# Both first modulation vectors formed on TensorE, x loaded by token groups, and value tiles moved behind their group's gated tiles

## The chip, the core and the metric

The kernel runs on one core of a Trainium2 chip. The metric is the device time of one execution in microseconds (us). Engines: PE is TensorE (matmuls), DVE is VectorE, ACT is ScalarE, POOL is GpSimd, SP is SyncE, which here only issues DMAs. ScalarE issues a few DMAs too.

## The reference, cut to what matters

One step of a two-layer trunk, in float32, on 128 context tokens and 1024 latent tokens (1152 columns together, feature-major). Each layer begins so:

```
def modulation(cond, w_mod, b_mod):
    m = jax.nn.silu(cond) @ w_mod + b_mod
    return jnp.split(m[:, None, :], 6, axis=-1)

def spatial_gating(uv, g_sgu, w_s, b_s):
    u, v = jnp.split(jax.nn.gelu(uv), 2, axis=-1)
    v = rmsnorm(v, g_sgu)
    ...
    return u * mixed.reshape(b, t, SGU_WIDTH)

def residual_block(x, mods, lp, mixer):
    sh1, sc1, g1, sh2, sc2, g2 = mods
    h = rmsnorm(x, lp['g_mix']) * (1 + sc1) + sh1
    mix, ctx_tensors = mixer(h)
    x = x + g1 * (mix @ lp['w_out'])
```

The normalised and modulated `h` goes through one input projection, whose columns feed neighbourhood attention, latent attention (`cq`, `ckv`, `krope`) and the spatial gating (`u`, `v`). A gated MLP with a depthwise convolution follows. The shift `sh1` and the scale `sc1` of layer 0 must exist before any `h` can be formed. There are two conditions, `c` for the latent tokens and `c_ctx` for the context tokens.

## The kernel before

The 1152 columns are three groups of 384 (G). A float32 product is made of three matmuls per 128-row chunk k (`mm3`, L183 to L185): high weights by high data, high by low, low by high. High parts are cast on ScalarE (L169), low parts are the residue, on VectorE (L171) or on POOL in pieces of 256 columns (L176). With 8 chunks a tile is 24 matmuls.

The opening. The two conditions come in as rows (`ccrow`), TensorE broadcasts them over 128 partitions (`ccb`, L1239), ScalarE applies silu. The shift vector is formed on VectorE: 16 products of 128 x 1024 with a sum along the row (`mod_tile`, L215). The scale vector is formed on TensorE: eight tiles of `wsc` (512 KB each) with a two-column weight (L1271), copied out by ScalarE (`mrow`), turned by eight small transposes (`pmT`). Then `norm_group` for the first group can start.

`norm_group` makes `h` for one group, chunk by chunk: in fused chunks VectorE forms `nt` (L342), ScalarE the high part (L344), VectorE the low one (L345); in the others VectorE (L337), ScalarE (L348, then the cast L169) and POOL (L176). The row factor `R` is statistics on TensorE (L297), a reciprocal root on VectorE (L270 to L278) and a broadcast on TensorE (L302). In layer 0 the squares of the next group (L288, L290) are formed inside the norm of a group.

The gating stage (`sgu`) comes next. For each group it makes two gated tiles (`pj`, weights by tokens, 128 x 384 each), whose gelu goes to `u` (L442). Then come nine value tiles (`pv`, tokens by weights, 128 x 320), three per group; their weights are cast by `tok_weights` to `twh` and `twl` in three loads (`win_v`). A value tile is drained by ScalarE (`vg`, L421, and a square, L423) and by VectorE (`kr`, L429) with POOL (L431). From the sixth value tile on in layer 0, the drain is followed by `mod_some`, products for the next modulation vectors (L235). The groups run in the order 1, 2, 0 in layer 0. In layer 1 the norms are formed in the feed-forward block before, and nothing is called between the tiles. The latent projections follow (`pj` again).

What sets the order: the program is written as below, and a scheduler of the framework then places each engine's instructions in a fixed sequence, by order of writing and by when operands and buffers are expected to be free; `issue_after` holds one instruction behind another. Each engine runs its sequence in order. Buffers come from pools with a fixed number of slots, so a load waits until the reader of the slot's last content is done: the third `win_v` load (L78) waits for the residue of the first. ScalarE's five DMA issues for the gating constants and the table of positions (L401 to L410) stand at the head of `sgu`.

## Time and profile before

| | |
|---|---|
| time, median of 3 runs | 3203.97 us (3203.35 to 3205.04) |
| the profiled execution's own time | 3203.48 us |
| its span in the trace | 3201.3 us |
| TensorE busy | 3114.0 us, 97% of the span |
| VectorE, ScalarE, POOL busy | 57%, 40%, 36% |
| layer 0: first gated matmul to first latent matmul | 45.92 to 119.58 us |
| layer 1: the same | 1628.49 to 1688.77 us |

Times in the rows are counted from the start of the span. A row of a timeline gives the start, the duration, the engine, the line, the operation with what it writes and reads, a count where equal neighbours are put together, and in brackets how long the engine was idle before and what released it. A "granted clock" of 1.00 is TensorE's 2.4 GHz level, 0.50 its 1.2 GHz level; a value between them is a mean over the stretch. An f32 matmul has two records in a count.

### The profile page before, as it was taken

Reading aid. Unit: us, or ns where it says so; the run is one execution under the profiler, and the core shown is the slowest. Engines: PE = TensorE matmul, PEld = TensorE weight load, DVE = VectorE, ACT = ScalarE, POOL = GpSimd, SP = SyncE. Lnnn points to the kernel's source line nnn. Section 1 sums busy time; section 2 is a strip of 40 time slices with the busy share of each in tenths; the row PEclk is TensorE's granted clock in tenths of the full one; section 3 lists DMA queues with packets and bytes.
Section 4 is the critical chain, followed back from the end, with each engine's and each line's share of the span. In section 5 each row is a group of like instructions: output and inputs, shape, how many; then the busy total and the mean of one; then the engine's idle time right before and its main releaser. Section 6 shows DMA issues by size and latency. Waiting matters only on the chain.

```text
span 3201.3 us, 50596 instructions
## 1 busy us (share of the span) xinstructions
PE 3114.0 (97%) x19298; PEld 2961.3 (93%) x19298; DVE 1812.7 (57%) x4908; ACT 1290.5 (40%) x2374; POOL 1155.9 (36%) x1359
## 2 busy tenths in 40 slices
...
GB/s 228 70 152 156 32 10 8 57 122 102 70 82 67 76 82 66 83 78 71 87 100 31 143 93 21 10 19 44 93 36 45 40 44 38 50 42 40 47 40 74
DMA packets 100504, 219.97 MB, mean 69 GB/s; under 512 B 25346, under 2 KB 41890, under 8 KB 100260
## 3 DMA queue, kind: packets, MB, share of 16 engines
...
## 4 chain that ended last, share of the span: by engine, by line
PE 88%; DVE 4%; issue 2%; POOL 2%; ACT 2%; DMA 1%; SPq 0%; DVEq 0%; ACTq 0%; POOLq 0%
PE f L184 11%; PE f L185 11%; PE f L183 11%; PE o L183 6%; PE o L184 6%; PE o L185 5%; PE O L538 5%; PE T L515 5%; PE pj L184 3%; PE pj L183 3%; PE pj L185 3%; PE S L959 2%; PE S L960 2%; PE S L961 2%; PE wo L183 1%
## 5 line engine op out<-in xcount | busy, mean ns | idle before, releaser
L176 POOL TENSOR_TENSOR whl<-wraw,whl 128x256 fp32r<-128x256 f32 (+1 forms) x704 | 549.9, 810 | 1090.6 <-ACT whl L169 883.3
L1090 DVE SCALAR_TENSOR_TENSOR acc<-f,vec,acc 128x1 f32<-128x1 f32 (+3 forms) x1056 | 397.4, 413 | 578.1 <-ACT acc L1086 566.6
L184 PE MATMUL f<-h,whl 128*128 128x384 f32 x2112 | 707.4, 335 | 3.9 <-POOL h L176 3.4
L185 PE MATMUL f<-h,whl 128*128 128x384 f32 x2112 | 706.4, 335 | 0.0
L183 PE MATMUL f<-h,whl 128*128 128x384 f32 x2112 | 705.7, 335 | 0.0
L184 PEld LDWEIGHTS f<-h,whl 128*128 128x128 f32 x2112 | 396.9, 188 | 7.2 <-POOL h L176 5.7
L183 PEld LDWEIGHTS f<-h,whl 128*128 128x128 f32 x2112 | 396.7, 188 | 0.6 <-ACT h L169 0.6
L185 PEld LDWEIGHTS f<-h,whl 128*128 128x128 f32 x2112 | 397.0, 188 | 0.0
L1076 DVE SCALAR_TENSOR_TENSOR x<-o,mod,x 128x384 f32<-128x384 f32 (+2 forms) x512 | 250.9, 514 | 205.6 <-PE o L185 204.8
L169 ACT CAST whl<-wraw 128x1024 fp32r<-128x1024 f32 (+3 forms) x204 | 190.7, 935 | 394.7 <-PE o L185 312.9
L183 PE MATMUL o<-ah,whl 128*128 128x384 f32 x912 | 304.7, 334 | 0.0
L185 PE MATMUL o<-ah,whl 128*128 128x384 f32 x912 | 304.7, 334 | 0.0
L184 PE MATMUL o<-al,whl 128*128 128x384 f32 x912 | 304.7, 334 | 0.0
L1086 ACT ACTIVATE acc<-f,vec 128x384 f32<-128x384 f32 x264 | 175.8, 668 | 156.5 <-PE f L185 151.2
L169 ACT CAST ah<-acc 128x383 fp32r<-128x383 f32 x132 | 67.5, 514 | 410.5 <-POOL acc L1133 410.5
L235 DVE SCALAR_TENSOR_TENSOR junk<-wmh,sc 128x512 bf16<-128x512 f32 x256 | 222.1, 868 | 7.7 <-DMA wmh<-wmodT 3.2
L515 PE MATMUL T<-cst,P 128*128 128x128 f32 x1504 | 201.5, 274 | 1.0 <-ACT P L707 1.0
L1133 POOL TENSOR_TENSOR acc<-acc 128x383 f32<-128x383 f32 x132 | 141.1, 1069 | 149.3 <-DVE acc L1090 149.3
L515 PEld LDWEIGHTS T<-cst,P 128*128 128x128 f32 x1504 | 174.8, 141 | 15.8 <-issue 5.7
L184 PE MATMUL pj<-h,whl 128*128 128x384 f32 x528 | 179.7, 341 | 5.7 <-POOL h L176 3.5
L965 ACT ACTIVATE P<-P,mx 128x1152 f32<-128x1152 f32 x128 | 161.4, 1261 | 55.7 <-DVE mx L962 55.3
L526 ACT COPY PT<-T 128x512 f32<-128x512 f32 (+1 forms) x288 | 154.1, 577 | 70.7 <-PE T L515 70.0
...
## 6 DMA issues: line engine op xcount, KB each, us to landing
...
wmh<-wmodT SPq DMA_DIRECT2D x128, 256.0 KB, 2.8
...
```

What stands on the lines that cost most here:

```text
L169: self.last_hi = self.nc.scalar.copy(hi, src)
L176: self.nc.gpsimd.tensor_tensor(out=lo[:, c], in0=src[:, c], in1=hi[:, c].bitcast(F32), op=ALU.subtract)
L183: mm(ps, wh(k), xh(k), start=(i == 0), stop=False)
L184: mm(ps, wh(k), xl(k), start=False, stop=False)
L185: mm(ps, wl(k), xh(k), start=False, stop=(i == last))
L235: self.nc.vector.scalar_tensor_tensor(out=self.junk[:, 0:512], in0=raw, scalar=1.0, in1=self.sc[c][:, o:o + 512], op0=ALU.mult, op1=ALU.mu ...
L515: nc.tensor.transpose(Tt[:, b * 128:(b + 1) * 128], u["P"][s][:, pc:pc + 128], self.I)
L538: nc.tensor.matmul(u["O"][64 * grp:64 * grp + 64, o0:o0 + n], w, src, start=(u["nop"][grp] == 1), stop=(u["nop"][grp] == u["tot"][grp]))
L965: nc.scalar.activation(out=P, in_=P, func=AF.Exp, bias=mx[:, 2:3], scale=-1.0, accum_out=mx[:, 3:4])
L1076: i = self.nc.vector.scalar_tensor_tensor(out=x[:, c0:c1], in0=ps[:, c0 - g * G:c1 - g * G], scalar=self.m(l, chunk, m, cond), in1=x[:, c0 ...
L1086: nc.scalar.activation(out=acc[:, c:c + G], in_=ps[:, 0:G], func=AF.Identity, scale=w(1), bias=vec[:, V_CB + ft:V_CB + ft + 1])
L1090: return nc.vector.scalar_tensor_tensor(out=acc[:, d:d + n], in0=p[:, s:s + n], scalar=w(i), in1=acc[:, d:d + n], op0=ALU.mult, op1=ALU.add)
```

## The change

Four things are done. The condition's vector is padded with zeros to 32 columns (`ctp`), and both vectors are formed on TensorE, from 16 tiles of 512 KB, with 64 matmuls of 32 x 256 outputs; two copies (ScalarE and VectorE) and four 128 x 128 transposes bring them into columns; `mod_tile` goes. The broadcasts of the conditions are issued after the twelfth tile. `x` is held in three tiles for each group (`XGroup`), group 1 loaded first and group 0 when the first norm has been written; the squares and the row factor of the next group are written after the first value tile of a group (`next0`). And in `sgu`, in both layers, the three value tiles of a group follow its two gated tiles, with the weights' casts written after the first group's gated tiles.

```diff
@@ -124,6 +124,17 @@
         return self._unit(g, k, 1)
 
 
+class XGroup:
+
+
+    def __init__(self, tile, off):
+        self.t, self.off = tile, off
+
+    def __getitem__(self, ix):
+        p, c = ix
+        return self.t[p, c.start + self.off:c.stop + self.off]
+
+
 class Wide:
     def __init__(self, hh, hl):
         self.hh, self.hl = hh, hl
@@ -208,14 +220,6 @@
             nc.scalar.dma_start(out=t, in_=bass.AP(tensor=cc.tensor, offset=cc[i].offset, ap=[[0, 128], [1, 1024]]))
             nc.scalar.activation(out=t, in_=t, func=AF.Silu)
             self.sc.append(t)
-
-    def mod_tile(self, l, t, conds, raw):
-        nc = self.nc
-        for c in conds:
-            i = nc.vector.scalar_tensor_tensor(
-                out=self.junk[:, 0:1024], in0=raw, scalar=1.0, in1=self.sc[c], op0=ALU.mult, op1=ALU.mult,
-                accum_out=self.mpart[:, t, c:c + 1])
-        return i
 
     def mod_half(self, l, n, first, end, buf):
         total = 2 * (end - first)
@@ -431,18 +435,21 @@
                 nc.gpsimd.tensor_tensor(out=self.krtok[:, t, :], in0=r[:, 0:32], in1=r[:, 32:64], op=ALU.add)
             if l == 0 and i >= MOD_FROM:
                 self.mod_some(ins)
+            return end
         for j, g in enumerate(order):
-            if j == 2:
-                W = self.tok_weights(3, 320)
             if norm:
-                norm(g)
+                norm[0](g)
             for i in range(2):
                 ps = self.anybank("pj")[:, 0:G]
                 self.wx(ps, Ws[i], f, g)
                 nc.scalar.activation(out=u[i][:, g * G:(g + 1) * G], in_=ps, func=AF.Gelu_apprx_tanh)
+            if j == 0:
+                W = self.tok_weights(3, 320)
+            for i in range(3):
+                ins = vtile(3 * j + i)
+                if norm and j < 2 and i == 0:
+                    norm[1](g, ins)
         norm = None
-        for i in range(9):
-            vtile(i)
         sm = self.st("sm")
         nc.vector.tensor_scalar(out=sm[:, 0:9], in0=ss[:, 0:9], scalar1=1.0 / 256, scalar2=None, op0=ALU.mult)
         y = self.rsqrt(sm[:, 0:9], 9, self.bank("rsq"))
@@ -1231,84 +1238,78 @@
         for c in range(2):
             nc.sync.dma_start(out=row[c][0:1, 0:1024], in_=io["cc"][c:c + 1, :])
         nc.sync.dma_start(out=self.cst, in_=io["cst"])
-        self.sc = [self.ptp.tile([128, 1152], F32, tag="pt", name="sc")[:, 0:1024] for _ in range(2)]
-        for c in range(2):
-            for j in range(2):
-                ps = self.sbank("ccb")
-                cs = slice(j * 512, (j + 1) * 512)
-                nc.tensor.matmul(ps, self.I[0:1, 0:1].to_broadcast([1, 128]), row[c][0:1, cs], start=True, stop=True)
-                nc.scalar.activation(out=self.sc[c][:, cs], in_=ps, func=AF.Silu)
-        row = None
-        x = [self.slot("x") for _ in range(8)]
+        ct = self.st("ct")
+        nc.sync.dma_start(out=ct[:, 0:16], in_=io["ccT"])
+        xg = {}
 
         def load_x(g):
+            t = [self.slot("xg") for _ in range(3)]
+            xg[g] = [XGroup(t[k // 3], (k % 3 - g) * G) for k in range(8)]
             for k in range(8):
                 cs = slice(g * G, (g + 1) * G)
-                nc.sync.dma_start(out=x[k][:, cs], in_=io["xT"][k, :, cs])
-        raws = []
-        for t in range(8):
-            r = self.slot("wmraw")[:, 0:1024]
-            nc.sync.dma_start(out=r, in_=io["wmodT"][0, t])
-            raws.append(r)
-            if t == 3:
-                load_x(1)
-        ct = self.st("ct")
-        nc.sync.dma_start(out=ct[:, 0:16], in_=io["ccT"])
-        nc.scalar.activation(out=ct[:, 16:32], in_=ct[:, 0:16], func=AF.Silu)
-        self.sq_begin()
-        for c in range(2):
-            for t in range(8):
-                last = self.mod_tile(0, t, (c,), raw=raws[t])
-        raws = None
-        for k in range(8):
-            self.sq_add(k, x[k], 1, nc.gpsimd)
-        pm = self.sbank("pm")
-        q4 = [slice(32 * j, 32 * j + 2) for j in range(4)]
-        for k in range(8):
-            r = self.slot("wmraw")[:, 0:1024]
-            nc.sync.dma_start(out=r, in_=io["wsc"][k])
-            for j in range(4):
-                nc.tensor.matmul(pm[q4[j], 0:256], ct[:, 16 + 2 * k:18 + 2 * k], r[:, j * 256:(j + 1) * 256],
-                                 start=(k == 0), stop=(k == 7))
-            if k == 0:
-                R1 = self.bank("R")
-                y = self.rstd_col(self.sumsq[:, G:2 * G], 0, R1)
-            if k in (5, 6):
-                self.W._load(k - 5)
+                nc.sync.dma_start(out=xg[g][k][:, cs], in_=io["xT"][k, :, cs])
+        load_x(1)
         for l in range(L):
             nc.sync.dma_start(out=self.vec[l], in_=io["vecs"][l])
-        self.bcast(R1, y)
-        R = {1: R1[:, 0:G]}
+        ctp = self.tmp("ctp")[:, 0:256].rearrange("p (k x) -> p k x", x=32)
+        nc.gpsimd.memset(ctp, 0.0)
+        nc.scalar.activation(out=ctp[:, :, 0:2], in_=ct[:, 0:16].rearrange("p (k c) -> p k c", c=2), func=AF.Silu)
+        self.sq_begin()
+        for k in range(8):
+            self.sq_add(k, xg[1][k], 1, nc.vector)
+        R1 = self.bank("R")
+        R = {1: self.rstd(self.sumsq[:, G:2 * G], 0, R1)}
+        pm = [self.bank("pm") for _ in range(2)]
+        for k in range(8):
+            for ch in range(2):
+                r = self.slot("wmraw")[:, 0:1024]
+                nc.sync.dma_start(out=r, in_=io["wsc"][k, :, ch * 1024:(ch + 1) * 1024])
+                for j in range(4):
+                    i = nc.tensor.matmul(pm[ch][32 * j:32 * j + 32, 0:256], ctp[:, k], r[:, j * 256:(j + 1) * 256],
+                                         start=(k == 0), stop=(k == 7))
+            if k == 5:
+                self.sc = [self.ptp.tile([128, 1152], F32, tag="pt", name="sc")[:, 0:1024] for _ in range(2)]
+                with self.tc.issue_after(i.ins):
+                    for c in range(2):
+                        for j in range(2):
+                            ps = self.sbank("ccb")
+                            cs = slice(j * 512, (j + 1) * 512)
+                            nc.tensor.matmul(ps, self.I[0:1, 0:1].to_broadcast([1, 128]), row[c][0:1, cs],
+                                             start=True, stop=True)
+                            nc.scalar.activation(out=self.sc[c][:, cs], in_=ps, func=AF.Silu)
+        row = None
+        self.W._load(1)
         load_x(2)
-        load_x(0)
         pt = self.obank("pmT")
-        for j in range(4):
-            if j % 2 == 0:
-                row = self.tmp("mrow")
-            o = j % 2 * 256
-            nc.scalar.copy(row[0:2, o:o + 256], pm[q4[j], 0:256])
-            for i in range(2):
-                nc.tensor.transpose(pt[:, 4 * j + 2 * i:4 * j + 2 * i + 2], row[0:2, o + i * 128:o + (i + 1) * 128],
-                                    self.I[0:2, 0:2])
-        with self.tc.issue_after(last.ins):
-            nc.vector.tensor_copy(self.mpart[:, 8:16, :].rearrange("p a b -> p (a b)"), pt[:, 0:16])
-        self.mod_finish(0, 0, 2)
+        mrow = self.tmp("mrow")
+        nc.scalar.copy(mrow[:, 0:256], pm[0][:, 0:256])
+        nc.vector.tensor_copy(mrow[:, 256:512], pm[1][:, 0:256])
+        for i in range(4):
+            nc.tensor.transpose(pt[:, i * 128:(i + 1) * 128], mrow[:, i * 128:(i + 1) * 128], self.I)
+        for c in range(2):
+            for ch in range(2):
+                ji = lambda a: a.rearrange("p (j i) -> p j i", i=2)
+                src = pt[:, ch * 256:(ch + 1) * 256].rearrange("p (i j x) -> p j i x", j=4, x=32)[:, :, :, c]
+                nc.vector.tensor_tensor(out=ji(self.mod[0][:, 8 * ch:8 * ch + 8, c]), in0=src,
+                                        in1=ji(self.vec[0][:, V_BM + 8 * ch:V_BM + 8 * ch + 8]), op=ALU.add)
+            nc.vector.scalar_tensor_tensor(out=self.a1[0][:, :, c], in0=self.mod[0][:, 8:16, c], scalar=1.0,
+                                           in1=self.vec[0][:, V_GM:V_GM + 8], op0=ALU.add, op1=ALU.mult)
         self.mt, self.mod_in = 0, []
         self.xdram = self.dp.tile([8, 128, T], F32, name="xdram")
         f = Feat(self)
-        xs = {g: x for g in range(3)}
-
-        x = None
 
         def norm0(g, f=f):
-            x = xs.pop(g)
-            self.norm_group(x, 0, self.a1[0], 0, g, f, R.pop(g))
-            if g:
-                n = {1: 2, 2: 0}[g]
-                for k in range(8):
-                    self.sq_add(k, x[k], n, nc.gpsimd if k in (1, 3, 5) else nc.vector)
+            self.norm_group(xg.pop(g), 0, self.a1[0], 0, g, f, R.pop(g))
+            if g == 1:
+                load_x(0)
+
+        def next0(g, behind):
+            n = {1: 2, 2: 0}[g]
+            for k in range(8):
+                self.sq_add(k, xg[n][k], n, nc.gpsimd if k in (1, 3, 5) else nc.vector)
+            with self.tc.issue_after(behind):
                 R[n] = self.sq_rstd(n, self.bank("R"))
-        f = [(f, norm0)]
+        f = [(f, (norm0, next0))]
         for l in range(L):
             x, f = self.mixer(l, f)
             f = self.ffn(l, x, f)
@@ -1351,7 +1352,7 @@
     d["wmodT"] = a["w_mod"].transpose(0, 2, 1).reshape(L, 48, 128, 1024)
     d["cc"] = np.stack([a["c"][0], a["c_ctx"]])
     d["ccT"] = d["cc"].reshape(2, 8, 128).transpose(2, 1, 0).reshape(128, 16)
-    d["wsc"] = a["w_mod"][0][:, 1024:2048].reshape(8, 128, 1024)
+    d["wsc"] = a["w_mod"][0][:, 0:2048].reshape(8, 128, 2048)
     d["vecs"] = np.stack([np.concatenate(
         [_cols(a["g_mix"][l]), _cols(a["g_ffn"][l]), _cols(a["g_cq"][l]), _cols(a["g_ckv"][l]),
          _cols(a["ffn_conv_b"][l])] + [_cols(a["ffn_conv_w"][l, i]) for i in range(3)]
```

How the instructions move, at three places.

ScalarE in the opening, before, from the first cast of a gated tile's weights (`whl`) to the fused steps of the first norm:

```order
L169 CAST whl<-wraw 128x1024
L401 DMA misc<-wsT 128x512
L404 DMA misc<-bs 64x2x128 x2
L408 DMA misc<-gsgu 128x256
L410 DMA tabk<-tabk 128x512
L169 CAST whl<-wraw 128x1024
L1289 COPY mrow<-pm 2x256 x4
L288 ACTIVATE sumsq<-x 128x384
L288 ACTIVATE sq<-x 128x384 x2
L344 ACTIVATE h<-nt,mod_96 128x384
L288 ACTIVATE sq<-x 128x384
```

And in the changed kernel, from the silu of the broadcasts (`sc`):

```order
L1279 ACTIVATE sc<-ccb 128x512 x4
L1285 COPY mrow<-pm 128x256
L180 CAST whl<-wraw 128x1024 x2
L352 ACTIVATE nt<-nt,mod_96,a_0_100 128x384
L292 ACTIVATE sumsq<-xg 128x384
L405 DMA misc<-wsT 128x512
L408 DMA misc<-bs 64x2x128 x2
L412 DMA misc<-gsgu 128x256
L414 DMA tabk<-tabk 128x512
L348 ACTIVATE h<-nt,mod_96 128x384
L180 CAST h<-nt 128x384
```

The two casts stand behind the copy of the vectors (`mrow`), and the five DMA issues, between the casts before, stand now between the first norm step with its square and the first high part `h`.

VectorE in layer 0, before, from the last step of the second group's row factor (`ry`) to its norm:

```order
L276 SCALAR_TENSOR_TENSOR R<-R,ry 128x3
L277 TENSOR_TENSOR R<-R,ry 128x3
L278 SCALAR_TENSOR_TENSOR ry<-R,ry 128x3
L342 SCALAR_TENSOR_TENSOR nt<-x,a_0_100,R 128x384
L337 TENSOR_TENSOR nt<-x,R 128x384
L342 SCALAR_TENSOR_TENSOR nt<-x,a_0_100,R 128x384
L290 TENSOR_TENSOR sumsq<-sumsq,sq 128x384
L345 SCALAR_TENSOR_TENSOR h<-nt,mod_96,h 128x384
L337 TENSOR_TENSOR nt<-x,R 128x384
```

And in the changed kernel:

```order
L280 SCALAR_TENSOR_TENSOR R<-R,ry 128x3
L281 TENSOR_TENSOR R<-R,ry 128x3
L282 SCALAR_TENSOR_TENSOR ry<-R,ry 128x3
L433 TENSOR_TENSOR kr<-pv,tabk 128x64 x2
L346 SCALAR_TENSOR_TENSOR nt<-xg,a_0_100,R 128x384
L341 TENSOR_TENSOR nt<-xg,R 128x384
L346 SCALAR_TENSOR_TENSOR nt<-xg,a_0_100,R 128x384
L349 SCALAR_TENSOR_TENSOR h<-nt,mod_96,h 128x384
L341 TENSOR_TENSOR nt<-xg,R 128x384
```

Two drains of value tiles (`kr`) stand ahead of the second group's norm; before, all nine come behind the third group's norm.

TensorE in layer 1, before: the end of the last of six gated tiles (the second of the last group, `pj_16132`) and the first value tiles (`pv`):

```order
L183 MATMUL pj_16132<-h_15937,whl_15970 128x384
L184 MATMUL pj_16132<-h_15937,whl_15970 128x384
L185 MATMUL pj_16132<-h_15937,whl_15970 128x384
L183 MATMUL pv_16158<-twh_16090,h_15573 128x320
L183 MATMUL pv_16188<-twh_16090,h_15573 128x320
L183 MATMUL pv_16219<-twh_16090,h_15573 128x320
L184 MATMUL pv_16158<-twl_16091,h_15573 128x320
L185 MATMUL pv_16158<-twh_16090,h_15573 128x320
```

And in the changed kernel: the end of the fourth gated tile (the first of the last group, `pj_16305`) and what follows; `pj_16186` is the second gated tile of the second group:

```order
L196 MATMUL pj_16305<-h_15945,whl_15978 128x384
L194 MATMUL pj_16305<-h_15951,whl_15978 128x384
L195 MATMUL pj_16305<-h_15951,whl_15978 128x384
L196 MATMUL pj_16305<-h_15951,whl_15978 128x384
L194 MATMUL pv_16068<-twh_16052,h_15587 128x320
L194 MATMUL pv_16098<-twh_16052,h_15587 128x320
L194 MATMUL pv_16129<-twh_16052,h_15587 128x320
L194 MATMUL pj_16186<-h_15638,whl_15984 128x384
L195 MATMUL pv_16068<-twl_16053,h_15587 128x320
L196 MATMUL pv_16068<-twh_16052,h_15587 128x320
```

Four gated tiles stand ahead of the value tiles in place of six; the second tiles of the second and of the last group (`pj_16186`, `pj_16331`) come behind them.

## Rows read from the trace of the kernel before

**Rows 1.** The page: the span, and the chain that ended last by engine.

```profile
span 3201.3 us, 50596 instructions
...
PE 88%; DVE 4%; issue 2%; POOL 2%; ACT 2%; DMA 1%; SPq 0%; DVEq 0%; ACTq 0%; POOLq 0%
```

**Rows 2.** The timeline of TensorE, in the opening and at the end of layer 0's gating stage.

```profile
3.49 7.16 PE L1239 MATMUL ccb<-ccrow,cst 1*128 1x512 f32 x8 [3.49 <-DMA cst<-cst]
...
25.09 5.17 PE L1271 MATMUL pm<-wmraw,ct 128*2 128x256 f32 x48
...
39.28 1.88 PE L1271 MATMUL pm<-wmraw,ct 128*2 128x256 f32 x16
...
45.92 0.69 PE L183 MATMUL pj<-h,whl 128*128 128x384 f32 x1 [2.73 <-ACT h L344]
...
119.58 0.34 PE L183 MATMUL pj<-h,whl 128*128 128x384 f32 x1
```

**Rows 3.** The timeline of VectorE, in the opening and in layer 0's gating stage.

```profile
44.62 0.60 DVE L342 SCALAR_TENSOR_TENSOR nt<-x,a,R 128x384 f32<-128x384 f32 x1
...
69.59 1.42 DVE L171 TENSOR_TENSOR twl<-wraw,twh 128x960 fp32r<-128x960 f32 x1
...
75.26 0.83 DVE L171 TENSOR_TENSOR twl<-wraw,twh 128x640 fp32r<-128x640 f32 x1 [1.23 <-ACT twh L169]
76.63 0.74 DVE L342 SCALAR_TENSOR_TENSOR nt<-x,a,R 128x128 f32<-128x128 f32 x2 [0.55 <-PE R L302]
...
92.03 0.22 DVE L429 TENSOR_TENSOR kr<-pv,tabk 128x64 f32<-128x64 f32 x1 [5.94 <-ACT vg L421]
...
106.33 0.68 DVE L235 SCALAR_TENSOR_TENSOR junk<-wm,sc 128x512 bf16<-128x512 f32 x1
```

**Rows 4.** The timeline of ScalarE, in the same stretch; ACTq rows are its DMA issues.

```profile
28.36 1.05 ACT L169 CAST whl<-wraw 128x1024 fp32r<-128x1024 f32 x1 [7.90 <-DMA wraw<-win_f]
28.37 0.39 ACTq L401 DMA_DIRECT2D misc<-wsT  x1
...
30.92 0.34 ACTq L410 DMA_DIRECT2D tabk<-tabk  x1
31.31 1.04 ACT L169 CAST whl<-wraw 128x1024 fp32r<-128x1024 f32 x1 [1.90 <-DMA wraw<-win_f]
...
45.25 0.61 ACT L344 ACTIVATE h<-nt,mod 128x384 fp32r<-128x384 f32 x1 [1.24 <-DVE nt L342]
...
91.61 0.38 ACT L421 ACTIVATE vg<-pv 128x256 f32<-128x256 f32 x1 [0.57 <-PE pv L185]
```

**Rows 5.** The waits of TensorE from 1628 to 1690 us (layer 1's gating stage): line, what it waited for, us in total, times, longest.

```profile
PE pj L184 <- POOL h L176: 0.2, 1, 0.2
```

**Rows 6.** Windows of TensorE: stretch, its length, busy time (records), granted clock, DMA share, GB/s.

```profile
26.00:30.00 4.00, 4.00 (x44) 1.00 1.03 410
50.00:52.00 2.00, 2.00 (x7) 0.50 0.00 0
54.00:56.00 2.00, 1.55 (x11) 1.00 0.00 0
```

**Rows 7.** A window of all engines in the opening: stretch, length, busy time of PE, PEld, DVE, ACT and POOL with their records, granted clock, DMA share, GB/s.

```profile
20.00:30.00 10.00, 6.28 (x54) 2.93 (x54) 7.59 (x15) 1.51 (x3) 4.11 (x3) 1.00 1.03 410
```

**Rows 8.** The timeline of TensorE in layer 1's gating stage.

```profile
1642.50 0.34 PE L185 MATMUL pj<-h,whl 128*128 128x384 f32 x1
...
1645.62 0.33 PE L185 MATMUL pj<-h,whl 128*128 128x384 f32 x1
...
1651.00 0.44 PE L184 MATMUL pj<-h,whl 128*128 128x384 f32 x1 [0.19 <-POOL h L176]
...
1656.66 0.59 PE L183 MATMUL pv<-twh,h 128*128 128x320 f32 x3
1657.19 0.42 PE L184 MATMUL pv<-twl,h 128*128 128x320 f32 x1
...
1688.77 0.34 PE L183 MATMUL pj<-h,whl 128*128 128x384 f32 x1
```

**Rows 9.** The timelines of VectorE, ScalarE and SyncE's queue in the same stage, put in order of time.

```profile
1642.60 0.62 DVE L342 SCALAR_TENSOR_TENSOR nt<-x,a,R 128x384 f32<-128x384 f32 x1 [1.10 <-PE R L302]
...
1652.14 1.28 ACT L442 ACT_TABLE_LOAD   x1 [1.25 <-issue]
...
1653.43 1.64 ACT L442 ACTIVATE u<-pj 128x384 f32<-128x384 f32 x4
...
1654.93 1.02 ACT L169 CAST twh<-wraw 128x960 fp32r<-128x960 f32 x1
...
1655.98 2.43 DVE L171 TENSOR_TENSOR twl<-wraw,twh 128x960 fp32r<-128x960 f32 x2 [5.91 <-ACT twh L169]
...
1657.17 0.33 SPq L78 DMA_DIRECT2D wraw<-win_v  x1
...
1660.17 0.73 ACT L169 CAST twh<-wraw 128x640 fp32r<-128x640 f32 x1 [2.56 <-DMA wraw<-win_v]
...
1660.93 0.83 DVE L171 TENSOR_TENSOR twl<-wraw,twh 128x640 fp32r<-128x640 f32 x1 [2.52 <-ACT twh L169]
```

**Rows 10.** The timeline of POOL: the last low part of layer 0's third norm, and of layer 1's last norm.

```profile
86.57 1.01 POOL L176 TENSOR_TENSOR h<-nt,h 128x384 fp32r<-128x384 f32 x1 [0.76 <-ACT h L169]
...
1649.68 2.30 POOL L176 TENSOR_TENSOR h<-nt,h 128x384 fp32r<-128x384 f32 x2 [1.91 <-ACT h L169]
```

7 lines of the change are left out of this document (4 added, 3 removed).

## The prediction, made before the changed kernel had run

> **What bounds the kernel now.** I read the page first. The span is 3201.3 us, and the chain of waits puts 88% of it on TensorE [rows 1]; so whatever delays TensorE's stream anywhere is a delay of the end, and what is saved on VectorE or ScalarE counts only where TensorE waits for them. Then the windows of TensorE for its clock, the timelines of the opening, of layer 0's gating stage and of layer 1's gating stage, and last the waits of TensorE in layer 1.
>
> Opening: the first gated matmul starts at 45.92 [rows 2]. Before it VectorE forms the shift vector, and the scale vector's tiles are done only at 39.28 + 1.88 = 41.2. The first normalised tile starts on VectorE at 44.62, its ScalarE step at 45.25 [rows 3, 4]. Layer 0's stage, from the first gated matmul to the first latent matmul at 119.58 [rows 2], takes 73.66 us. In layer 1 TensorE never stands still: over 62 us it waits 0.2 us for POOL and hardly more in all [rows 5]. The same order of stage thus costs much in layer 0 and nothing in layer 1.
>
> The clock matters in the opening. The granted clock reads 1.00 (2.4 GHz) in 26 to 30 us and 0.50 (1.2 GHz) in 50 to 52, and it is back at 1.00 in 54 to 56, after a stretch in which TensorE was busy 2.00 of 2.00 us [rows 6]. Yet the scale tiles ran 6 in 5.17 us (0.86 each) at a granted 1.00 and 2 in 1.88 (0.94 each) at 0.50 [rows 2]: the same pace. So the opening ran at the lower level from its first matmul, whatever the column says before 32 us. The Trainium skill (TensorE: Matmul & The Clock Gate, section "What's actually happening") says that the slow state is the default and that activity lifts it; the trace agrees, with 0.86 beside 0.94. By the column alone my opening would come out some 6 us earlier than by this rule; I carry both as ends below, from the rows.
>
> **The change, part by part.**
>
> *Opening.* Removed: 16 products on VectorE, four broadcasts at the start, the small transposes. Added: 16 tiles of 512 KB in place of 8 + 8, so 64 matmuls of 256 columns instead of 32, and the four broadcast matmuls (7.16 us [rows 2]) moved to stand behind the twelfth tile. DMA runs at 410 GB/s [rows 7], so a tile takes 1.28 to 1.31 us. The second weight tile's cast starts at 31.31 [rows 4]; by the bytes in front of it (10.6 MB before; 10.3 MB ahead of the last vector tile now) the last vector tile lands near 30.7, the two weight tiles near 32.0 and 33.3, and the twelfth vector tile near 25.4.
> At the low level: last matmul of tile 12 at 26.2, broadcasts until 33.4, three tiles at 0.86 to 36.0, copy, transposes and the last tile to 38.8, four small VectorE steps, so the norm starts at 39.9 instead of 44.62. But ScalarE now does the vector's copy, two casts of 1.04, one step of the norm and a square, and then issues five DMAs before its first norm tile. In the trace these five take from 28.37 to 31.26, 2.9 us, in front of a cast that waited for its transfer [rows 4]; now they stand in front of the first operand. First gated matmul: 36.5 + 0.4 copy, casts to 38.4, norm step (behind VectorE's, 40.9) to 41.6, square and issues to 44.9, operand 0.7: 45.6. The early norm is given back; the gain is 0.3.
> At the high level everything on TensorE halves: broadcasts end near 29.4, the last tile is done soon after it lands, the norm starts near 33.0. Now the weight tiles' landing holds ScalarE: casts to 34.3, then step, square and issues to 38.2, and the first gated matmul at about 39.2. The gain is 6.7.
> I take the middle, 42.4 and a gain of 3.5: the same broadcasts ran wholly at the low level before, but with an idle engine ahead of them instead of twelve tiles, and no row shows what comes after such tiles.
> At nothing I cost these: the squares of the first group, now on VectorE, lie under the 20 us in which the vector tiles arrive; x keeps its number and size of loads, and group 0's, now behind the first value weights on SP's queue, are wanted only by the third norm, 30 us later (were they late, that norm would wait); the statistics of the next group are held back behind a value tile on purpose, and only that group's norm is queued behind them.
>
> *Layer 0's stage.* The norm's chain paces the first tile of each group; the second follows. One gated tile is 24 matmuls at 3.12 / 18 = 0.173 [rows 8], 4.16 us. A value tile is 24 at (1688.77 - 1657.19) / 212 = 0.149 [rows 8], 3.57, three 10.7. Without the next group's squares in it, a norm takes what it takes in layer 1: from 1642.60 to 1649.68 + 2.30 = 1651.98 [rows 9, 10], 9.4 us; in the third group from 76.63 to 86.57 + 1.01, 10.95 [rows 3, 10].
> First group: 9.4 - 1.3 (norm start to first matmul) + 0.3 + 4.16 = 12.5. Then TensorE meets the value weights, which until now were cast under the third group's tiles. Last gelu and cast 0.4 + 1.0, with handover 1.75; the residue of 1.42 [rows 3] less the three matmuls that need only the cast, 1.05; second pair 0.3; the third load is issued only when the first residue has freed its buffer, and from that residue's end (69.59 + 1.42 = 71.01) to the end of the third one (75.26 + 0.83 = 76.09) [rows 3] it is 5.1 us, of which 17 matmuls and some fillers cover 3.0: 2.1. Together 5.2. Then value tiles 10.7, statistics 1.6. The next norm starts only when VectorE has drained the group's last value tile, since the drains stand ahead of it: gelu 0.38 and its handover, product 0.22 [rows 3, 4], first norm pair 0.6 + 0.6, handover: 2.1 us of idle TensorE. Second group 9.4 + 0.7 = 10.1, values 10.7, statistics 1.6. Before the third group two 0.68 products [rows 3] stand in the way too: 2.1 + 1.4 = 3.5. Third group 10.95 + 0.65 = 11.6, values 10.7, and 1.3 off for value and second-tile matmuls that fill gaps. Sum: 12.5 + 5.2 + 10.7 + 1.6 + 2.1 + 10.1 + 10.7 + 1.6 + 3.5 + 11.6 + 10.7 - 1.3 = 79.0, against 73.66: a loss of 5.3. Layer 0 net: -3.5 + 5.3 = +1.8 (from -1.4 to +5.0).
>
> *Layer 1's stage.* It gains nothing from the opening and gets the new order too. Before, six gated tiles (25 us) stand in front of the first value matmul at 1656.66. While the fifth waits on the last norm (done 1651.98) and the sixth runs, ScalarE issues its DMAs, loads its table (1652.14, 1.28), drains four tiles (1653.43, 1.64) and casts the value weights (1654.93); the residue comes at 1655.98, and TensorE meets it 0.2 us late [rows 8, 9]. Now only four gated tiles stand in front, the fourth being the last group's, which still waits for the same norm: TensorE is through at about 1652.3. The casts follow two drains instead of four, 0.82 us less, and no third drain in between: first value matmul at about 1655.3, 1.36 earlier than before. But two tiles, 2 x 4.16 = 8.3 us, are still to be done: 8.3 - 1.36 = 6.9 lost. Residue at 1656.45, less the four matmuls that can go before it: 0.55. The third load comes over SP's queue after the first residue (issue 1657.17, cast 1660.17, residue 1660.93 + 0.83 [rows 9], all some 1.2 earlier now): 0.1 + 0.3 + 0.2 behind the matmuls that stand there. Sum 8.1; from 6 (should the scheduler's fillers cover the residues and ScalarE's drains come up sooner) to 9.5 (should the third load be as late as in layer 0).
>
> Elsewhere nothing changes, and TensorE has no slack to take the loss back: the end shifts with it. Sum: 1.8 + 8.1 = 9.9 on the profiled execution, 3201.3 + 2.2 outside the span = 3203.5, so 3213.4; the median of the runs is 3203.97, within 0.5 of it. I say 3213.5.
>
> **Rivals.**
> 1. *The opening pays for it (no change).* High level, and the five DMA issues overlap the norm, because they are issued while ScalarE waits for VectorE: first gated matmul at 36.5, gain 9.4. Layer 0 is then -9.4 + 5.3 = -4.1, layer 1 +6 to +8: 3205.4 to 3207.4. For it: the first issue at 28.37 runs beside the cast that started at 28.36 [rows 4]. Against: only one; in layer 1 ScalarE's table load comes 1.25 us late, with nothing but issues in front of it [rows 9].
> 2. *Faster.* The value weights' casts are ready before the gated tiles end: if the stalls in front of the value tiles fall below 1 us in both layers, layer 0 keeps its gain of -9.4 with 5.3 - 4.2 = 1.1 lost, and layer 1 loses none of 8.1: 3195 to 3196. It decides as soon as the cast of the first value weights starts by about 1651 in layer 1. Against: it stands behind the table load, which in the trace begins at 1652.14 [rows 9], and behind two gelus of tiles that end at 1652.3.
> 3. *Worse.* The low level lasts through the opening and comes back in the idle stretches that the new order makes in layer 0 (2 to 5 us each, where the trace shows the drop to 0.50 after an opening in which TensorE stood idle for long [rows 2, 6]). The value tiles and gated matmuls behind each such stretch then run some microseconds at half pace: +5.0 + 8.1, and 2 to 4 more: 3216.6 to 3220.6. Against: the 2.73 us ahead of 45.92 were already at the low level, so no row shows a drop by so short a gap.
>
> **How the numbers follow.** My case 0.50, the first rival 0.22, the second 0.08, the third 0.20. A difference of 0.2%, 6.4 us, is about what a measurement can tell from no change; so slower means above 3210.4. My case spans 3210 to 3217 and gives 0.45 slower and 0.05 no change; the third adds 0.20 slower, the first 0.22 no change less 0.02 either way, and 0.02 of the second ends there too: faster 0.07, same 0.27, slower 0.66. The range takes in my case, most of the third and of the first: 3204 to 3220; 0.08 of the second and a little at either end lie outside.
>
> **What would show it.** In the changed kernel: TensorE idle for some 3 us in front of layer 1's first value matmul, released by ScalarE's cast of the value weights, and 48 gated matmuls behind it; about 5 us in front of and inside layer 0's first value tile; 2 and 3.5 us before its second and third groups; the first gated matmul between 39 and 46, released by ScalarE, with five DMA issues just in front. The broadcasts' duration (7.2 or 3.6 us) tells the clock. It is wrong if the first gated matmul comes before 38, or if TensorE in layer 1 waits under 3 us between the fourth gated tile and the end of the first value tile.

## The result, and the profile after

The changed kernel takes 3223.41 us (median of 4 runs, 3220.30 to 3224.35); the kernel before, beside it, 3203.66 (4 runs, 3202.37 to 3205.04). The ratio is 1.0061, with a 95% interval of 1.0049 to 1.0073: slower by 19.7 us. The forecast said slower by 9.5 to 3213.5, with a range up to 3220: the direction is right, the size half, and the time lies outside the range. Two disturbed executions are left out below, one of the kernel before and one, the only one with a trace, of the experiment with the issues behind the fourteenth vector tile.

The page of the changed kernel: span, and the chain that ended last by engine.

```profile
span 3218.4 us, 50680 instructions
...
PE 88%; DVE 4%; issue 2%; ACT 2%; POOL 2%; DMA 1%; SPq 0%; ACTq 0%; DVEq 0%; POOLq 0%
```

Against [rows 1] the shares of the chain are the same and the span is 17.1 us longer. (The profiled execution, 3220.30, is the shortest of the four.) So the page can't say where the time went; five anchors on TensorE can. Timeline of TensorE, changed kernel: the first gated matmul, the first latent matmul of layer 0, the first gated matmul of layer 1, its first value matmul, its first latent matmul.

```profile
48.05 1.01 PE L194 MATMUL pj<-h,whl 128*128 128x384 f32 x2 [6.06 <-ACT h L348]
...
127.50 0.34 PE L194 MATMUL pj<-h,whl 128*128 128x384 f32 x1
...
1639.67 0.33 PE L194 MATMUL pj<-h,whl 128*128 128x384 f32 x1
...
1666.42 0.71 PE L194 MATMUL pv<-twh,h 128*128 128x320 f32 x3 [2.60 <-ACT twh L180]
...
1708.67 0.34 PE L194 MATMUL pj<-h,whl 128*128 128x384 f32 x1
```

Before, these are 45.92, 119.58 [rows 2], 1628.49, 1656.66 and 1688.77 [rows 8]. So the first gated matmul comes 48.05 - 45.92 = 2.1 us later (forecast: 3.5 earlier). Layer 0's stage takes 127.50 - 48.05 = 79.45, not 73.66: 5.8 more (forecast 5.3). From there to layer 1 it loses 3.3 more (1512.17 against 1508.91), where nothing had been forecast. Layer 1's stage takes 1708.67 - 1639.67 = 69.00, not 60.28: 8.7 more (forecast 8.1). The rest gives 2.8 back, in small steps that I have not followed up. The two stages came out as worked out; the opening did not.

*The opening.* Timeline of TensorE, changed kernel (pm: the vector tiles from the ninth to the twelfth, ccb: the broadcasts).

```profile
24.75 0.64 PE L1268 MATMUL pm<-wmraw,ctp 128*32 128x256 f32 x8 [0.63 <-DMA wmraw<-wsc]
26.03 1.08 PE L1268 MATMUL pm<-wmraw,ctp 128*32 128x256 f32 x8 [0.65 <-DMA wmraw<-wsc]
...
28.59 1.08 PE L1268 MATMUL pm<-wmraw,ctp 128*32 128x256 f32 x8 [0.20 <-DMA wmraw<-wsc]
29.60 7.19 PE L1277 MATMUL ccb<-ccrow,cst 1*128 1x512 f32 x8
```

And windows of all engines (stretch, length, busy time of PE, PEld, DVE, ACT and POOL with their records, granted clock, DMA share, GB/s), first two of the kernel before, then those of the changed kernel.

```profile
4.00:8.00 4.00, 4.00 (x6) 1.44 (x5) 0.09 (x1) 1.19 (x2) 0.00 (x0) 1.00 1.00 385
8.00:12.00 4.00, 2.65 (x4) 0.56 (x2) 3.90 (x7) 1.91 (x4) 0.00 (x0) 1.00 1.04 388
```

```profile
4.00:8.00 4.00, 0.00 (x0) 0.00 (x0) 1.12 (x2) 2.64 (x5) 0.00 (x0) 1.00 0.94 278
8.00:12.00 4.00, 0.00 (x0) 0.00 (x0) 2.79 (x5) 2.59 (x5) 0.00 (x0) 1.00 1.01 309
...
24.00:26.00 2.00, 0.75 (x12) 0.16 (x8) 0.00 (x0) 0.00 (x0) 0.00 (x0) 0.95 1.03 422
26.00:28.00 2.00, 1.77 (x16) 0.40 (x16) 0.00 (x0) 0.00 (x0) 0.00 (x0) 0.50 1.03 416
...
30.00:34.00 4.00, 4.00 (x5) 1.42 (x5) 0.00 (x0) 1.18 (x2) 0.00 (x0) 0.50 1.02 402
34.00:38.00 4.00, 4.00 (x16) 1.26 (x18) 0.00 (x0) 1.21 (x3) 0.00 (x0) 0.50 0.95 334
```

Three things are to be seen. From 4 to 12 us the loads move at 278 and 309 GB/s, where the kernel before moved 385 and 388; at the 410 of [rows 7] these 8 us would have moved 0.93 MB more, 2.3 us of transfer. That is most of the 3.2 us by which the twelfth tile is late: it is there at 28.6, not near 25.4. `x` heads the queue in this stretch, but that is not the reason, as an experiment below shows. From 18 to 26 us a tile runs in 0.64 us, at the upper level (2.4 GHz), and TensorE waits as long for the next one; at 26 the granted clock falls to 0.50 (1.2 GHz) and a tile takes 1.08, three tiles ahead of the broadcasts. And these take 7.19 us, as at the start of the kernel before [rows 2]. The Trainium skill (TensorE: Matmul & The Clock Gate, section "What's actually happening") says that activity lifts the slow state; this stretch does not bear it out: TensorE counts as busy all the time from 30 to 38 us and the granted clock stays at 0.50.

Then ScalarE, changed kernel; ACTq is its queue of DMA issues:

```profile
44.33 0.71 ACT L352 ACTIVATE nt<-nt,mod,a 128x384 f32<-128x384 f32 x1 [2.49 <-DVE nt L341]
44.37 0.40 ACTq L405 DMA_DIRECT2D misc<-wsT  x1
...
46.89 0.44 ACTq L414 DMA_DIRECT2D tabk<-tabk  x1
47.38 0.61 ACT L348 ACTIVATE h<-nt,mod 128x384 fp32r<-128x384 f32 x1 [1.93 <-issue]
```

The five issues stand from 44.37 to 47.33 in front of the first operand, 2.96 us (2.9 forecast).

*Layer 0's stage.* Timeline of TensorE, changed kernel: the first gated matmul of the second group and of the third; and a window of all engines in the first group's value tiles.

```profile
81.12 0.61 PE L194 MATMUL pj<-h,whl 128*128 128x384 f32 x2 [1.97 <-ACT h L348]
...
106.92 0.62 PE L194 MATMUL pj<-h,whl 128*128 128x384 f32 x2 [3.47 <-ACT h L348]
...
64.00:68.00 4.00, 4.00 (x15) 4.00 (x16) 2.76 (x3) 2.05 (x5) 1.75 (x2) 0.50 0.64 138
```

*Layer 1.* Timeline of TensorE in the first value tile, then of ScalarE, then the windows, changed kernel.

```profile
1667.61 0.64 PE L195 MATMUL pv<-twl,h 128*128 128x320 f32 x1 [0.31 <-DVE twl L182]
...
1668.31 0.47 PE L194 MATMUL pv<-twh,h 128*128 128x320 f32 x1
1668.58 0.47 PE L195 MATMUL pv<-twl,h 128*128 128x320 f32 x1
```

```profile
1663.32 1.28 ACT L445 ACT_TABLE_LOAD   x1 [1.25 <-issue]
1664.62 0.87 ACT L445 ACTIVATE u<-pj 128x384 f32<-128x384 f32 x2
1665.38 0.99 ACT L180 CAST twh<-wraw 128x960 fp32r<-128x960 f32 x1
```

```profile
1668.00:1670.00 2.00, 2.00 (x9) 2.00 (x9) 0.84 (x1) 0.04 (x1) 0.00 (x0) 0.50 0.68 161
1670.00:1672.00 2.00, 2.00 (x12) 2.00 (x11) 0.52 (x1) 0.73 (x1) 0.00 (x0) 0.75 0.86 222
```

The wait is the one forecast: table load, two drains, cast of the value weights, and TensorE idle for 2.60 us. What follows it was not in my sum: the value matmuls behind the wait start every 0.27 us instead of the 0.149 of the prediction, at a granted 0.50, until 1671. The first value matmul starts 1666.42 - 1639.67 = 26.75 after the stage, 1.42 earlier than before (1.36 forecast). In the gated tiles ahead of it TensorE also waits 1.8 us for POOL and 0.8 for VectorE, where it waited 0.2 before [rows 5]: the fourth tile can't end before the last norm does. The waits of TensorE from 1639.7 to 1708.7 us (line, what it waited for, us in total, times, longest):

```profile
PE pj L195 <- POOL h L187: 1.8, 2, 0.9
```

*Between the layers.* Of the 3.3 us there 2.4 lie at a single place: the two kernels are 8.75 us apart at the first pair of rows below and 11.19 at the next matmul of that kind (811.88 against 800.69). At about 800 us TensorE waits for a norm in both kernels, equally long; the timeline and the windows around it, first of the changed kernel, then of the kernel before:

```profile
804.27 1.41 PE L301 MATMUL R<-cst,sumsq 128*128 128x1 f32 x6 [2.26 <-DVE nt L341]
...
800.00:805.00 5.00, 2.74 (x16) 2.45 (x14) 2.73 (x7) 3.10 (x8) 3.84 (x5) 0.90 0.31 102
805.00:810.00 5.00, 5.00 (x18) 5.00 (x18) 3.58 (x13) 1.98 (x4) 3.78 (x5) 0.50 0.01 4
```

```profile
795.52 0.80 PE L297 MATMUL R<-cst,sumsq 128*128 128x1 f32 x6 [2.26 <-DVE nt L337]
...
792.00:797.00 5.00, 2.74 (x19) 2.45 (x18) 2.83 (x8) 3.11 (x7) 3.09 (x4) 1.00 0.38 108
797.00:802.00 5.00, 4.68 (x29) 4.36 (x28) 2.90 (x16) 1.24 (x3) 4.08 (x5) 1.00 0.00 0
```

The same wait of 2.26 us: the clock falls behind it in one execution and not in the other. The change did nothing to this code. Of the 13 kernels with a trace here it falls in three, the changed kernel, the one with layer 1 in the old order and the one with the opening alone, and not in three others with that opening and the new order.

### The profile page after: what moved, and what is told of

It reads as the page before. It is cut to its first block, busy times and chain, and to the rows that moved or that the text cites. A ratio compares the mean times of both kernels' runs of the same rounds, so it can differ in the third digit from the quotient of the medians.

```text
span 3218.4 us, 50680 instructions
## 1 busy us (share of the span) xinstructions
PE 3129.9 (97%) x19358; PEld 2973.2 (92%) x19358; DVE 1796.7 (56%) x4885; ACT 1291.6 (40%) x2371; POOL 1141.0 (35%) x1353
## 4 chain that ended last, share of the span: by engine, by line
PE 88%; DVE 4%; issue 2%; ACT 2%; POOL 2%; DMA 1%; SPq 0%; ACTq 0%; DVEq 0%; POOLq 0%
PE f L195 11%; PE f L196 11%; PE f L194 11%; PE o L194 5%; PE o L195 5%; PE o L196 5%; PE O L545 5%; PE T L522 5%; PE pj L194 3%; PE pj L195 3%; PE pj L196 3%; PE S L966 2%; PE S L967 2%; PE S L968 2%; PE wo L194 1%
## 5 line engine op out<-in xcount | busy, mean ns | idle before, releaser
L194 PE MATMUL pj<-h,whl 128*128 128x384 f32 x528 | 179.9, 343 | 11.8 <-ACT h L348 11.5
L522 PEld LDWEIGHTS T<-cst,P 128*128 128x128 f32 x1504 | 174.8, 141 | 15.7 <-issue 5.7
L195 PE MATMUL pj<-h,whl 128*128 128x384 f32 x528 | 180.1, 343 | 3.9 <-POOL h L187 3.1
```

The costliest lines, as they stand in the source:

```text
L194: mm(ps, wh(k), xh(k), start=(i == 0), stop=False)
L195: mm(ps, wh(k), xl(k), start=False, stop=False)
L522: nc.tensor.transpose(Tt[:, b * 128:(b + 1) * 128], u["P"][s][:, pc:pc + 128], self.I)
```

## The experiments

Times are medians; the intervals are of the ratio to the kernel before. That kernel, run beside each, had medians from 3203.16 to 3204.15. Its own runs spread over 5 to 8 us, those with the new opening in the old order over 8 to 12. No kernel leaves work out; the last two add matmuls that nothing reads.

**Which part costs what.** Three kernels take the change apart: the changed kernel with layer 1 in the old order (below); with both layers in the old order (`new` is then false in both), so that only the opening is new; and the kernel before with the lines of `sgu` and of the norms from the change.

```diff
+        new, early = l in (0,), l in ()
         for j, g in enumerate(order):
+            if (not new and j == 2) or (early and j == 0):
+                W = self.tok_weights(3, 320)
...
+            if not new:
+                continue
             for i in range(3):
                 ins = vtile(3 * j + i)
...
+        for i in range(0 if new else 9):
+            vtile(i)
```

> The changed kernel with layer 1's gating stage in the order of before (all gated tiles, then the value tiles); opening and layer 0 stay changed. Theory A (the new order itself takes two gated tiles, 8.3 us, out of the cover over the value weights' casts in layer 1): layer 1's stage, first gated to first latent matmul, falls back from 69.0 to about 60.3 us, and the time from 3223.4 to about 3214.7. Rival B (layer 1 only pays for things that come later from the opening, or for TensorE's clock): the stage stays above 66 us and the time above 3220.

> The changed kernel with the order of before in both layers, so the new opening alone. Theory A: the first gated matmul stays near 48.0 (2.1 later than before's 45.92), the rest is as before: about 3206, up to 3208.5 should TensorE's clock fall once more near 800 us. Rival C (the new opening gains and only the order loses): first gated matmul before 44 and 3200 or less.

> The kernel before with the new order in both layers, so the order alone. Theory A: layer 0's stage 73.7 + 5.8 = 79.5 us, layer 1's 69.0, together 3203.7 + 5.8 + 8.7 = 3218.2, up to 3221 with one more fall of the clock. Rival C': the order costs this only behind the new opening, 3212 or less.

Measured: layer 1 in the old order 3213.28 (8 runs; 1.0026, 1.0016 to 1.0037); opening alone 3208.69 (10 runs, 3204.07 to 3215.60; 1.0018, 1.0008 to 1.0027); order alone 3218.36 (4 runs; 1.0046, 1.0031 to 1.0061). With 3204.15 for the kernel before beside them the order alone costs 14.2 us and the opening alone 4.5; their sum, 18.7, is 1.0 short of the 19.7 of both. The trace of the order alone has layer 0's stage at 79.30 us (46.29 to 125.59) and layer 1's at 68.61 (1635.45 to 1704.06), close to the changed kernel's 79.45 and 69.00: the two stages lose their time with the old opening too. Step by step it is 4.5 for the opening, 4.6 for layer 0's order (3213.28 - 3208.69) and 10.6 for layer 1's (19.7 less the 9.1 of the first kernel). My terms were -3.5, +5.3 and +8.1. In the first kernel layer 1's value matmuls start without a wait, and the stage takes 1701.17 - 1641.08 = 60.09, as before. Timeline of TensorE there:

```profile
1641.08 0.33 PE L194 MATMUL pj<-h,whl 128*128 128x384 f32 x1
...
1669.26 0.59 PE L194 MATMUL pv<-twh,h 128*128 128x320 f32 x3
...
1701.17 0.34 PE L194 MATMUL pj<-h,whl 128*128 128x384 f32 x1
```

**The five issues.**

```diff
-        nc.scalar.dma_start(out=misc[:, 0:512], in_=io["wsT"][l])
+        nc.sync.dma_start(out=misc[:, 0:512], in_=io["wsT"][l])
```

(and the other four alike)

> The changed kernel with the five DMA issues at the head of the gating stage moved from ScalarE to SyncE. Theory A (the issues stand in front of the first operand in the opening and in front of the table load in layer 1): first gated matmul 2.9 us earlier, near 45.1; layer 1's first value matmul about 1.2 earlier in its stage; 3223.4 - 4.1 = 3219. Rival D (POOL's low parts of the weights, done at 46.5, hold the first tile, and SyncE's queue brings the third value load later): 3222 to 3225.

Measured 3219.94 (4 runs; 1.0050, 1.0035 to 1.0065): 15.8 above the kernel before, 3.9 less than the changed kernel, by intervals that overlap. Layer 1's stage took 67.74 instead of 69.00 and its first value matmul came 1.3 us earlier, with ScalarE's table load at 1660.83, right behind the norm's last cast, where it had waited 1.25 for the issues. But the first gated matmul came at 48.54, no earlier: with the issues gone, squares of the next group moved in front of the first operand. This run doesn't show the issues' price in the opening.

**Layer 1's weights earlier.** In layer 1 the casts of the value weights are written ahead of the first gated tiles.

```diff
+        new, early = l in (0, 1), l in (1,)
         for j, g in enumerate(order):
+            if (not new and j == 2) or (early and j == 0):
+                W = self.tok_weights(3, 320)
...
-            if j == 0:
+            if j == 0 and not early:
                 W = self.tok_weights(3, 320)
```

> The changed kernel with layer 1's value weights cast before its first gated tiles in the program text; in the sequence of ScalarE the three casts then stand behind the norm and the DMA issues, but in front of the table load and the gelus. Theory A (in the cover that is left, the first value tile waits for whatever comes last: casts, then the third load): first value matmul 2 us earlier in its stage, but the third load's wait takes its place: stage 67 to 69 us, 3221 to 3223. Rival J (only the casts' place behind the table load costs): stage 64 us or less, 3218.

Measured 3217.64 (4 runs, 3214.22 to 3223.32; 1.0045, 1.0030 to 1.0059): 13.5 above the kernel before (3204.14 beside it and the next three), 6.2 less than the changed kernel, by intervals that overlap. Layer 1's stage, 66.82 instead of 69.00, explains 2.2 of it; its first value matmul comes 24.74 after the stage's start, 2.0 earlier, and TensorE doesn't wait for it. The stage is still 6.5 longer than before. So the wait for the weights is the smaller part: the first value matmul can come only 3.4 us earlier than in the kernel before (28.17 after the start), since the fourth tile waits for the last norm (1.8 us for POOL and 0.8 for VectorE, as in the changed kernel), and two tiles, 8.3 us, then stand behind it. In the profiled run the opening, whose code is the changed kernel's, reached its first gated matmul at 44.27 instead of 48.05. Timeline of TensorE there, the twelfth tile and the broadcasts:

```profile
28.63 0.64 PE L1277 MATMUL pm<-wmraw,ctp 128*32 128x256 f32 x8 [0.64 <-DMA wmraw<-wsc]
29.20 3.87 PE L1286 MATMUL ccb<-ccrow,cst 1*128 1x512 f32 x8
```

The tile lands at the same time as in the changed kernel, but the clock had not fallen, and the broadcasts take half as long. The same code thus has an opening of two lengths.

**The opening repaired, in the old order.** First the broadcasts go back to the start.

```diff
         nc.sync.dma_start(out=self.cst, in_=io["cst"])
+        for c in range(2):
+            for j in range(2):
+                nc.tensor.matmul(ps, self.I[0:1, 0:1].to_broadcast([1, 128]), row[c][0:1, cs],
+                                 start=True, stop=True)
...
-            if k == 5:
-                with self.tc.issue_after(i.ins):
```

> The new opening with the order of before in both layers (as a2_all_old, 3208.7), and the four broadcast matmuls at the start, as in before, in place of behind the twelfth vector tile. Theory E (the broadcasts at the low level stand 7.2 us in front of the last vector tiles, which had landed): last vector tile done near 35 instead of 41, norm 36.3, first gated matmul near 42 in place of 47.7: 3208.7 - 6 = 3202.7. Rival F (ScalarE's issues and the landing of the weight tiles hold the first operand whatever TensorE does): first gated matmul not before 45.5, 3206 or more.

Then, besides, layer 0's five issues after the first group's gated tiles:

```diff
-        nc.scalar.dma_start(out=misc[:, 0:512], in_=io["wsT"][l])
+        if l:
+            issue()
...
+            if j == 0 and l == 0:
+                issue()
```

> As o1_ccb_first, and layer 0's five DMA issues on ScalarE written behind the first group's gated tiles instead of at the head of the stage. Theory E: they stood in front of the first operand for 2.9 us: first gated matmul near 39, 3199.8. Rival G (POOL's low parts of the weights or the loads of x become the limit): gain under 1 us against o1_ccb_first.

Then, besides, `x` loaded behind the fourth vector tile:

```diff
-        load_x(1)
...
         for k in range(8):
+            if k == 2:
+                load_x(1)
```

> As o2_issue_late, and x of the first group loaded behind four vector tiles instead of in front of all. Theory H (x at the head of the queue moves at 260 to 330 GB/s in 4 to 12 us, where before moved 385, so the vector tiles land 3 us later): the last vector tile lands 1.5 to 3 us earlier, first gated matmul near 37, 3198. Rival I (the bytes are the same and only come in another order): landing of the last vector tile and first gated matmul as in o2_issue_late, within 0.7 us.

Measured: 3205.75 (10 runs, 3201.12 to 3209.52; 1.0004, 0.9995 to 1.0014), 3206.89 (10 runs; 1.0012, 1.0003 to 1.0022), 3207.18 (10 runs; 1.0010, 1.0001 to 1.0020). Moving the broadcasts gives 2.9 back, by intervals that overlap, and the opening then costs nothing that can be measured; the other two are some 3 us slower than the kernel before, by intervals just clear of no change. Nothing is gained, although the first gated matmul comes at 42.29, 40.31 and 39.34, up to 6.6 us earlier than before. Layer 0's first latent matmul comes at 119.42, 122.14 and 122.80, against 119.58.

The third of these kernels also tells whether `x` at the head of the queue slowed the loads. Its twelfth tile and two of its windows:

```profile
28.34 0.64 PE L1292 MATMUL pm<-wmraw,ctp 128*32 128x256 f32 x8 [0.41 <-DMA wmraw<-wsc]
```

```profile
4.00:8.00 4.00, 4.00 (x5) 1.42 (x5) 0.00 (x0) 2.41 (x4) 0.00 (x0) 1.00 0.93 283
8.00:12.00 4.00, 4.00 (x16) 1.26 (x18) 0.00 (x0) 1.21 (x3) 0.00 (x0) 1.00 0.98 321
```

The stretch from 4 to 12 us is as slow as with `x` at the head, and the twelfth tile comes at 28.34, against 28.41 and 27.71 in the two kernels ahead of it and 28.59 in the changed kernel. From 12 to 14 us, when nearly all packets are `x`'s, 394 GB/s move. So rival I holds for the landing, and `x` at the head is not what made the tiles late. All traces with the new opening have 277 to 360 GB/s in these two windows; the two with the old one have 385 and 388, and 362 and 375 (the order alone). Which part of the new opening does it was not tried; the two loads of `vec`, which moved from 27 to 6 us, are one candidate.

The windows of all engines between 54 and 66 us, first of the kernel with the broadcasts at the start, then of the kernel before:

```profile
54.00:58.00 4.00, 4.00 (x16) 4.00 (x16) 2.38 (x13) 2.56 (x4) 1.03 (x2) 0.58 0.01 2
...
62.00:66.00 4.00, 2.81 (x9) 2.01 (x9) 3.07 (x6) 3.97 (x9) 2.69 (x3) 0.77 0.01 4
```

```profile
54.00:58.00 4.00, 3.55 (x22) 3.06 (x21) 2.81 (x10) 2.36 (x5) 1.91 (x2) 1.00 0.00 0
...
62.00:66.00 4.00, 1.76 (x7) 1.18 (x8) 3.07 (x7) 3.56 (x8) 2.89 (x3) 1.00 0.00 0
```

With the early start TensorE is busy for all of 54 to 58 and does 16 records; the kernel before does 22 in less busy time. By 119 its lead of 3.6 is 0.2. The norm paces the first tile of a group in both; in the early kernel the clock then falls, and the second tile runs at half pace. With the issues moved there is a second reason. ScalarE there, in the kernel with `x` moved:

```profile
60.15 0.39 ACTq L406 DMA_DIRECT2D misc<-wsT  x1
...
62.60 0.45 ACTq L415 DMA_DIRECT2D tabk<-tabk  x1
63.10 0.61 ACT L348 ACTIVATE h<-nt,mod 128x384 fp32r<-128x384 f32 x1 [2.46 <-issue]
```

The issues took 2.9 us out of the second group's norm instead of the first's.

Two more of this kind: the issues behind the fourteenth vector tile, without and with `x` moved.

```diff
+            if k == 6:
+                with self.tc.issue_after(i.ins):
+                    self.pre = {0: self.gate_consts(0)}
```

> As o1_ccb_first (new opening, broadcasts at the start, order of before in both layers), and layer 0's five DMA issues on ScalarE placed behind the fourteenth vector tile, where ScalarE has nothing else to do. Theory K (an issue block costs 3 us wherever it stands in front of a group's norm: of the first group in o1_ccb_first, of the second in o2_issue_late, and its stall brings TensorE's clock down): first gated matmul near 40, no wait over 2.5 us in front of the second group, layer 0's stage back to 74 to 77 us, first latent matmul near 115; 3205.8 - 3 = 3202 or less. Rival L (layer 0's stage ends near 119.5 whatever the opening does, by the loads of x or by the norms' engines): first latent matmul not before 118.5, 3205 or more.

> As o4_issue_early, and x of the first group loaded behind four vector tiles. By o3_x_mid the first gated matmul comes 1 us earlier, and POOL's low parts hold the second chunk instead: within 1 us of o4_issue_early. If the order of loads matters (theory H), 2 us less.

Measured 3205.25 (10 runs; 1.0005, 0.9996 to 1.0014; no trace) and 3209.20 (11 runs; 1.0018, 1.0009 to 1.0027). In the second a load of the gated weights got ahead of the last two vector tiles on SyncE's queue, and the first gated matmul came at 44.00. Neither beats the kernel before.

**The clock held up.** Each vector tile is multiplied a second time into a bank that nothing reads, and 24 more such matmuls follow the transposes (20 in the second kernel): first in the kernel with the broadcasts at the start, then in the changed kernel.

```diff
+                for j in range(4):
+                    nc.tensor.matmul(dm[32 * j:32 * j + 32, 0:256], ctp[:, k], r[:, j * 256:(j + 1) * 256],
+                                     start=True, stop=True)
```

> As o1_ccb_first, and 88 matmuls whose result nobody reads: each vector tile's four are done twice, and 24 stand between the transposes and the first gated matmul, so that TensorE does not stand still there. Nothing else is added. Theory M (the opening's gain is lost to TensorE's clock: with gaps in its stream it goes back to 0.50, and the gated tiles behind run at 0.32 us a matmul in place of 0.17): granted clock 1.00 up to the first gated matmul at 42.3, no second tile at 0.32, layer 0's stage 72 to 74 in place of 77.1 and more in the slower runs; 3201 to 3203 in place of 3205.75, and the runs closer together. Rival N (the clock falls in the first gated tile anyway, which is paced by the norm, or it is not the clock): 3205 to 3207.

> The changed kernel with the same 84 unread matmuls in the opening (64 beside the vector tiles, 20 behind the transposes). Theory M: the broadcasts run in 3.6 to 4 us in place of 7.2, the first gated matmul comes near 44.5 in place of 48.05: 3223.4 - 3.5 = 3220. Rival N: the broadcasts stay at 7.2 or the stage behind takes it back: 3222 to 3225.

Measured 3203.92 (11 runs, 3200.38 to 3210.11; 1.0007, 0.9998 to 1.0016) and 3218.83 (5 runs, 3218.17 to 3220.81; 1.0053, 1.0041 to 1.0066). Against 3203.16 beside it the changed kernel is 15.7 slower with the extra work, 4.1 less than without, by intervals that overlap; its broadcasts take 5.2 us and the first gated matmul comes at 46.55. In the old order 0.8 is left over the kernel before, where it was 1.6 without the extra matmuls: no difference that these runs can tell. In the trace of the first, layer 0's stage runs from 41.93 to 124.18, 8.6 us longer than before, and the windows show why so little is gained:

```profile
34.00:38.00 4.00, 3.82 (x60) 1.88 (x56) 2.00 (x9) 2.27 (x3) 1.06 (x2) 1.00 0.96 342
...
40.00:44.00 4.00, 1.48 (x5) 1.09 (x6) 2.05 (x3) 2.73 (x6) 4.00 (x6) 0.89 0.80 239
44.00:48.00 4.00, 3.22 (x10) 2.04 (x9) 2.53 (x6) 3.21 (x8) 2.97 (x3) 0.69 1.00 351
...
56.00:60.00 4.00, 4.00 (x14) 4.00 (x14) 1.39 (x8) 0.60 (x2) 1.01 (x1) 0.50 0.00 0
```

The upper level lasts as long as the extra matmuls do, and is lost again where the norm paces TensorE.

## Why the prediction was right and wrong

*Layer 0's stage: right, in part by luck.* 79.45 against 79.0. Its idle stretches came as named: ScalarE's cast and the residue in front of the first value tile; 1.97 us of idle in front of the second group for the 2.1; 3.47 in front of the third for the 3.5. The 5.2 us around the first value tile came out otherwise: the third load's residue ended 5.5 after the first's (5.1 forecast), but TensorE stood idle for 2.5 in all and ran the rest at half pace (granted 0.50 from 64 to 68), which was in no term. Over the stage it was busy for 69.98 us, before for 66.82, with nearly the same records: of the 5.8 more some 3 are pace. By the runs it costs 4.6 for the 5.3, as a difference of two medians of kernels that spread.

*Layer 1's stage: right, its size 0.6 short.* 8.7 for 8.1. The 6.9 (two tiles less 1.36) came out, with 1.42 for the 1.36. The sign that I had set, no less than 3 us of waiting up to the end of the first value tile, was missed by a hair (2.60 + 0.31 = 2.91). The third load, which I gave 0.6, was covered; instead the clock fell in the wait. The twelve value matmuls from 1668.05 to 1670.98 started 0.12 us later each than at full pace, 1.4 us. That the two tiles are the main term, and not the wait for the weights, the run with the weights earlier bears out: without the wait 6.5 are left, of which 8.3 - 3.4 = 4.9 are the tiles. The run with layer 1 in the old order shows the stage at 60.09 and the time 10.6 lower.

*The opening: wrong, and this is the failed step.* I bounded the first gated matmul by 45.6 (low level) and 39.2 (high level) and took the middle, 42.4, a gain of 3.5. It came at 48.05, outside both bounds, and the opening alone cost 4.5 in the runs. That is 8.0 of the 9.9 between forecast and result. The term that failed is "the twelfth vector tile near 25.4": it was counted by bytes from the arrival of the second weight tile in the kernel before, so with that kernel's rates (385 and 388 GB/s from 4 to 12 us), and the new opening's loads ran at 278 and 309 there, so it came at 28.6. Why they ran slower stays open; the place of `x` in the queue is not the reason (28.34 with `x` further back). These 3.2 us shift both ends, to 42.4 and 48.8, and the forecast had only its best case left; the changed kernel's 48.05 and the five other traces with the broadcasts behind the twelfth tile (44.27 to 48.54) lie between the shifted ends. The rest of the low working held to 0.8: broadcasts 7.19 for 7.16, five issues 2.96 for 2.9. Second, I looked only at the start of the stage: with the same opening and the old order it begins 1.8 us late (47.73), and layer 0's stage takes 81.63 in place of 73.66 [rows 2] in the profiled run, the longest of its kernel. TensorE has the same 385 records in both stages and is busy for 73.93 us in place of 66.82, at a mean granted clock of 0.85 in place of 0.95. That an opening of this kind lengthens the stage behind it was in no term.

*Rival 1* needed the high level and issues that overlap the norm, and had neither. *Rival 2* needed the cast of the value weights by about 1651; on that scale it came at 1665.38 - (1639.67 - 1628.49) = 1654.2. *Rival 3*, at 0.20, was the other part of the truth: the low level lasted through the broadcasts, and value matmuls ran at half pace behind the idle stretches of layer 0 (granted 0.50 from 64 to 68) and, which it had not said, of layer 1. Its lower end was added up wrongly: 3203.5 + 5.0 + 8.1 is 3216.6 already, and with the 2 of its own it is 3218.6. Its upper end, 3220.6, lacks the 3.2 of the twelfth tile; with them it is 3223.8.

*What stays open.* Which part of the new opening slows its loads from 4 to 12 us. Why the same wait of 2.26 us near 800 us costs the clock in one execution and not in the other (single times of the opening alone differ: 3204.75 us at a mean granted clock of 0.989 and 3215.60 at 0.985). That the early start alone would pay if the norm did not pace the first tiles was argued, not tried, and so was filling layer 1's wait with unread matmuls. No version beat the kernel before.
